# The first feed-forward stage by seven products from its fifth m-tile on, and five modulation sections moved to other stages

## The chip, the cores and the metric

The kernel runs on one core of a Trainium2 chip. Its time is device microseconds of one execution; the kernel before took 2546.53 us (median of three runs, 2545.23 to 2547.19). TensorE multiplies, VectorE and ScalarE do elementwise work, GpSimd is a slower third engine for that, and SyncE (SP in the profile) issues all DMAs.

## The reference, cut to what matters

Two layers run over 640 tokens (128 of a context, 512 latent) of width 1024 in float32. Each layer has a feed-forward stage, a mixer (a recurrent head group and two kinds of attention) and a second feed-forward stage, each with a residual and a layer norm. Shift, scale and gate come from nine "modulation sections" a layer, each 1024 columns of one big matrix, for two condition vectors (one per token group):

```python
mod = (silu(cond) @ w_mod + b_mod)            # 9 sections of 1024 columns
x = layer_norm(ALPHA * x + 0.5*g1 * swiglu(x*(1+sc1)+sh1, lp, 0))
x = layer_norm(ALPHA * x + g2 * mixer(x*(1+sc2)+sh2))
x = layer_norm(ALPHA * x + 0.5*g3 * swiglu(x*(1+sc3)+sh3, lp, 1))
swiglu(u) = (silu(u @ w_gate) * (u @ w_up)) @ w_down     # 1024 -> 2816 -> 1024
```

## The kernel before, in words

**Tiling.** A feed-forward stage works through 22 m-tiles of 128 hidden columns. Every float32 matrix is split into a high and a low part, and a product is three matmuls (high by high, high by low, low by high). In the classic form an m-tile takes, for gate and for up, 8 blocks of the inner dimension by 2 halves of 320 tokens by 3 matmuls: 96 matmuls of 320 columns (`mtile`, the three lines 526 to 528). The down-projection takes groups of m-tiles ("chunks"): for each of 5 token tiles and 2 halves of the output, 3 matmuls of 512 columns per m-tile, 30 per m-tile in all.

**Two forms of the stage.** The first stage of layer 0 is made by `ffn_steps`, all classic, with chunks of 3, 3, 4, 4, 4, 4 (downs at lines 821 to 823). Its down multiplies each result by the gate on VectorE (L828) and adds it to x at once, on GpSimd (L830; VectorE in the last chunk). The three other stages are made by `ffn_fast`: `CLASSIC` = 3 classic m-tiles, and from then on seven products of 4 blocks each instead of eight (a Strassen-like scheme over token halves and inner halves), 7 x 4 x 3 = 84 matmuls per m-tile (L1083). For them VectorE and ScalarE first make sums of the input's quarters (`sums`: two rounds of 11 whole-tile VectorE instructions, high priority), and `third` replaces a quarter in place. Each m-tile's weights are combined and split by `prep` (L1051, L1055, L1059: 4 differences, 7 casts, 7 remainders), and the products' results are put together from six PSUM banks by L1107 to L1137. Downs come after every third m-tile (L1195 to L1197); the sums over m-tiles are gathered without the gate in five tiles `acc` (L1200 copies, then L1208 adds), and `blend`, shortly before the last down, multiplies them by the gate on GpSimd (L1167, ten times) and adds x, which had been written to memory (`x_d`) and is read back (L1165, L1169).

**The opening** is special to layer 0: `start` does m-tiles 0 and 1 while modulation sections 0 and 1 arrive, adding their shift later as a bias (`biased`, with L674 and L687). `start2` does m-tile 2 and between its blocks the eight steps of section 2, on TensorE. VectorE and ScalarE follow the written order until it ends.

**Modulation sections** come in two forms. On TensorE (`body`, L364): 8 steps, each a load of 512 KB and 4 matmuls (which the trace counts as 8 records). On VectorE (`vbody`): 8 steps with a load and 4 instructions each (L329 in the first step, else L331), and at the end matmuls that add over partitions (L340, 16 records). `PLAN` says which sections are made where: in the feed-forward stages by VectorE, in the mixers by TensorE (groups of `MODG` = 4 steps at given units of the attention, `mod_fill`; unit = one head by 128 queries). Eight are in the first stage, two in each mixer, one in each of the others.

**Order.** A stage is a list of `Step`s with loads, splits and a body. `run` traces them in order; at each `yield` of a body (a tick) it makes at most one split of the coming steps, feeds loads while fewer than `NR` = 7 raw buffers are out, and advances the background generators. In `ffn_fast` the sections' VectorE instructions are traced by the generator `trickle`, one per `MGAP` = 12 ticks. A product has 4 ticks, a down 10. A scheduler then orders each engine's instructions by their place in this trace, with `high_priority` moving some ahead; it may start a later instruction when its inputs are there.

Of the kernel before, what the change touches and what calls it, by code (L numbers as in the profile page):

```python
# [18 lines left out]
P = 128  # L19
D = 1024  # L20
KT = 8
# [62 lines left out]
MGAP = 12  # L84
# [3 lines left out]
def f(ap):  # L88
    return ap.bitcast(F32)
# [20 lines left out]
class Kern:  # L110
# [456 lines left out]
    def ffn_steps(self, l, j, mods):  # L567

        nc, I = self.nc, self.I
        env = {}  # L570
        S = []

        def B(dt=F32):
            return env["pool"].tile([P, TOK], dt, tag="B", bufs=11, name=self.nm("b"))

        def DW(shape):
            return env["pool"].tile(shape, F32R, tag="DW", bufs=8, name=self.nm("dw"))

        def T(shape):
            return env["pool"].tile(shape, F32, tag="T", bufs=3, name=self.nm("t"))  # L580

        def G4(shape):
            return env["pool"].tile(shape, F32, tag="G", bufs=4, name=self.nm("g"))

        jj = (0, 2)[j]
        hs = {}
        halves = {}
        dws = []
        for m in range(NM):
            g, u, d = {}, {}, {}  # L590
            fs = slice(m * P, (m + 1) * P)
            halves[m] = (g, u, d)

            def w_in_view(w):
                return w[l, j][:, fs].rearrange("(k p) f -> p k f", p=P)
# [3 lines left out]
            dl, dsp = self.weight(I["ffn_w_down"][l, j][fs, :], [P, D], d, DW)  # L599

            def silu(g, cut=HALF):
                for a, b in self.chunks(g["s"], g["ps"], cut):
                    nc.scalar.activation(a, b, AF.Silu)

            def hout(m, g, u, cut=HALF):
                s = g["s"]
                for a, b in self.chunks(s, u["ps"], cut):
                    nc.vector.tensor_mul(a, a, b)
                hh, hl = B(F32R), B(F32R)
# [4 lines left out]
            dws.append((dl, dsp))  # L614
            late_g, late_d = ((), ()) if m == 0 else LATE[l == 0 and j == 0].get(m, ((), (m,)))

            def gbody(m=m, g=g, late=[fn for i in late_g for fn in dws[i][1]]):
                g["ps"] = self.p2("pg")
                g["s"] = B()
                late = list(late)  # L620
                for c in range(2):
                    for _ in self.mtile(g["ps"], g, c):
                        yield
                        for _ in range(min(2, len(late))):
                            late.pop(0)()
                for fn in late:
                    fn()
                silu(g)


            def ubody(m=m, g=g, u=u, late=[fn for i in late_d for fn in dws[i][1]]):
                u["ps"] = self.p2("pu")
                if l == 0 and j == 0 and m == 4:
                    for i in range(DEPTH):
                        self.setup_vec(i)
                late = list(late)
                for c in range(2):
                    for _ in self.mtile(u["ps"], u, c):
                        yield
                        if late:  # L640
                            late.pop(0)()
                for fn in late:
                    fn()
                hout(m, g, u)

            def first(m=m, g=g, u=u):
                env["cm"] = self.tc.tile_pool(name=f"ffn{l}{j}", bufs=1, reuse_waits="tile")
                env["pool"] = env["cm"].__enter__()
                self.B_DW = DW
                g["ps"], u["ps"] = self.p2("pu"), self.p2()  # L650
                g["s"] = B()
                yield from self.mtile(g["ps"], g, 0, CUT)
                self.after_a()
                yield from self.mtile(u["ps"], u, 0, CUT)
                yield from self.mtile(g["ps"], g, 1, CUT)
                silu(g, CUT)
                yield from self.mtile(u["ps"], u, 1, CUT)
                hout(m, g, u, CUT)

            def biased(m, g, u):  # L660
# [29 lines left out]
                hh, hl = B(F32R), B(F32R)  # L690
                nc.scalar.copy(hh, s)
                nc.vector.tensor_sub(hl, s, f(hh))
                hs[m] = (hh, hl)
# [7 lines left out]
            def start(gsp, usp, g1=g, u1=u):  # L701


                g0, u0, _ = halves[0]
# [24 lines left out]
                env["cm"] = self.tc.tile_pool(name=f"ffn{l}{j}", bufs=1, reuse_waits="tile")  # L729
# [23 lines left out]
            def start2(m=m, g=g, u=u):  # L753
# [4 lines left out]
                for h, k0 in ((g, 0), (u, 0), (g, 4), (u, 4)):  # L758
                    if k0 and self.late_bias:
                        self.bg.append(self.late_bias.pop(0)())  # L760
                    for k in range(k0, k0 + 4):
                        self.block(h, k)
                        yield CAP2 if h is u and k >= 6 else 0
                        if not todo:
                            continue
                        st = todo.popleft()
                        while not st.ready():
                            self.feed()
                        for _ in st.body():
                            yield  # L770
# [1823 lines left out]
```

## Time and profile before

| | us |
|---|---|
| median of three runs | 2546.53 |
| the profiled execution | 2543.89 |
| its span | 2541.8 |
| first feed-forward stage, to the first matmul of the mixer | 537.1 |
| mixer of layer 0, to the first matmul of the next stage | 327.9 |

The page gives, for one profiled execution, the busy time of each engine, the waits and the costliest groups of instructions. PE is TensorE, PEld its weight load, DVE VectorE, ACT ScalarE, POOL GpSimd. A name like L1083 is a line of the kernel. Granted clock is the share of TensorE's full clock.

### The profile page before, as it was taken

What the parts mean: (1) busy time and instruction counts of PE and PEld (TensorE: products, weight loads), DVE (VectorE), ACT (ScalarE), POOL (GpSimd) and SP (SyncE); (2) the same over time, 40 slices, a digit from 0 to 9 for tenths busy, and PEclk for the clock granted to TensorE, in tenths of its full rate; (3) what the DMA queues carried; (4) which work ended last, traced back from release to release, by engine and by line L of the source; (5) the groups of instructions that cost most, each with busy time, mean ns of one, the idle gap of its engine ahead of it and who ended that gap; (6) DMA issues with size and microseconds to landing.
All of it is one profiled execution on the core that took longest, in us unless ns stands there. A gap on an engine that the chain in (4) does not pass through costs nothing. (4 is left out here: it accounts for less than half of the span.)

```text
span 2541.8 us, 39941 instructions
## 1 busy us (share of the span) xinstructions
PE 2443.6 (96%) x15804; PEld 2218.4 (87%) x15804; DVE 1891.1 (74%) x3161; ACT 1068.9 (42%) x1882; POOL 411.2 (16%) x389
## 2 busy tenths in 40 slices
PE   8899999999999999999999999999999999999997
PEld 7789898988867999999889999988987799999986
DVE  5887778687754797777789777778785578777777
ACT  3212111246674444343354434435657534433432
POOL 2320221113632100000200000020373210000022
PEclk9999999999999999999999999999999999999999
DMA  8655445522233233333333333332232323333321
GB/s 286 197 152 155 141 147 185 158 69 80 95 90 113 67 132 111 98 100 100 108 91 124 113 96 100 100 108 82 91 112 90 97 76 100 110 107 104 113 92 50
DMA packets 271394, 288.53 MB, mean 114 GB/s; under 512 B 13436, under 2 KB 223976, under 8 KB 271208
## 3 DMA queue, kind: packets, MB, share of 16 engines
q1 hardware_dynamic: 271208, 285.99, 36.3%
q8 instruction: 124, 2.03, 0.3%
q14 instruction: 62, 0.51, 0.1%
HBM read 268.17 MB, written 16.21 MB: 112 GB/s over the span
## 5 line engine op out<-in xcount | busy, mean ns | idle before, releaser
L1083 PE MATMUL pb<-u,w 128*128 128x320 f32 x2736 | 420.4, 309 | 1.7 <-DVE b L1129 1.7
L1083 PEld LDWEIGHTS pb<-u,w 128*128 128x128 f32 x2736 | 406.7, 188 | 4.0 <-issue 2.4
L526 PE MATMUL p<-u,w 128*128 128x320 f32 (+2 forms) x1104 | 348.3, 316 | 8.6 <-ACT u L517 6.4
L527 PE MATMUL p<-u,w 128*128 128x320 f32 (+2 forms) x1104 | 345.8, 314 | 1.8 <-DVE u L518 1.8
L528 PE MATMUL p<-u,w 128*128 128x320 f32 (+2 forms) x1104 | 344.4, 313 | 0.0
L1083 PE MATMUL pb<-s,w 128*128 128x320 f32 x2052 | 322.0, 309 | 1.3 <-ACT b L1136 1.3
L1083 PEld LDWEIGHTS pb<-s,w 128*128 128x128 f32 x2052 | 306.0, 188 | 3.7 <-ACT b L1136 1.9
L1055 ACT CAST w<-raw 128x512 fp32r<-128x512 f32 x399 | 239.8, 619 | 162.8 <-DVE raw L1051 107.5
L1059 DVE TENSOR_TENSOR w<-raw,w 128x512 fp32r<-128x512 f32 x399 | 272.6, 696 | 34.9 <-ACT w L1055 34.2
L194 ACT CAST dw<-raw 128x1024 fp32r<-128x1024 f32 x87 | 89.1, 1051 | 452.6 <-PE p L1196 263.9
L331 DVE SCALAR_TENSOR_TENSOR x<-raw,cst,x 128x512 f32<-128x512 f32 x308 | 236.9, 815 | 33.3 <-DMA raw<-in_w_mod 33.2
L1195 PE MATMUL p<-dw,b 128*128 128x512 f32 x630 | 249.7, 396 | 11.3 <-DVE x L1208 10.1
L1196 PE MATMUL p<-dw,b 128*128 128x512 f32 x630 | 245.8, 390 | 0.0
L1197 PE MATMUL p<-dw,b 128*128 128x512 f32 x630 | 245.5, 390 | 0.0
L526 PEld LDWEIGHTS p<-u,w 128*128 128x128 f32 x1104 | 211.5, 192 | 13.7 <-ACT u L517 7.4
L527 PEld LDWEIGHTS p<-u,w 128*128 128x128 f32 x1104 | 211.7, 192 | 2.9 <-DVE u L518 2.5
L528 PEld LDWEIGHTS p<-u,w 128*128 128x128 f32 x1104 | 211.1, 192 | 0.3 <-DVE w L199 0.3
L194 ACT CAST w<-raw 128x1024 fp32r<-128x1024 f32 x100 | 104.8, 1050 | 241.3 <-PE p L527 162.3
L1208 DVE TENSOR_TENSOR x<-x,p 128x512 f32<-128x512 f32 x150 | 102.8, 685 | 110.5 <-PE p L1197 110.5
L1195 PEld LDWEIGHTS p<-dw,b 128*128 128x128 f32 x630 | 118.2, 188 | 47.3 <-DVE x L1208 21.6
L199 DVE TENSOR_TENSOR w<-raw,w 128x1024 fp32r<-128x1024 f32 x100 | 124.1, 1242 | 44.6 <-ACT w L194 40.5
L1157 POOL TENSOR_SCALAR x<-x 128x1024 f32<-128x1024 f32 x6 | 6.3, 1056 | 871.1 <-PE p L1197 438.3
(367 smaller groups left out, 4815.7 us busy)
## 6 DMA issues: line engine op xcount, KB each, us to landing
raw<-in_w_mod SPq DMA_DIRECT2D x132, 512.0 KB
raw<-in_ffn_w_gate SPq DMA_DIRECT2D x88, 512.0 KB
raw<-in_ffn_w_up SPq DMA_DIRECT2D x88, 512.0 KB
raw<-in_ffn_w_down SPq DMA_DIRECT2D x88, 512.0 KB
raw<-in_w_in SPq DMA_DIRECT2D x26, 512.0 KB
xd<-x SPq DMA_DIRECT2D x25, 512.0 KB
raw<-in_w_out SPq DMA_DIRECT2D x16, 512.0 KB
t<-xd SPq DMA_DIRECT2D x30, 256.0 KB
```

The source lines that it names most:

```text
L194: nc.scalar.copy(h, hold["raw"])
L199: nc.vector.tensor_sub(l, hold["raw"], f(hold["hi"]))
L331: e.scalar_tensor_tensor(acc[:, cs], hold["raw"][:, cs], c, acc[:, cs], op0=ALU.mult, op1=ALU.add)
L526: nc.tensor.matmul(out, lhsT=wh, rhs=xh, start=start, stop=False)
L527: nc.tensor.matmul(out, lhsT=wh, rhs=xl, start=False, stop=False)
L528: nc.tensor.matmul(out, lhsT=wl, rhs=xh, start=False, stop=stop)
L1055: nc.scalar.copy(w[:, 0], at(src))
L1059: nc.vector.tensor_sub(w[:, 1], at(src), f(w[:, 0]))
L1083: nc.tensor.matmul(out, lhsT=a1, rhs=b1, start=(start and k == 0 and i == 0), stop=(k == 3 and i == 2), skip_group_check=not start,)
L1195: nc.tensor.matmul(pt, lhsT=hh[:, ts], rhs=d["hi"][:, cs], start=(i == 0), stop=False)
L1196: nc.tensor.matmul(pt, lhsT=hh[:, ts], rhs=d["lo"][:, cs], start=False, stop=False)
L1197: nc.tensor.matmul(pt, lhsT=hl[:, ts], rhs=d["hi"][:, cs], start=False, stop=(i == len(ms) - 1))
```

## The change

`ffn_steps` goes. Its special parts for m-tiles 0 to 2 become `opening`, and the first stage is now made by `ffn_fast` too, with four classic m-tiles (`classic = CLASSIC + opens`), so from m-tile 4 on by seven products. The order at the start is: `start`; `third` (m-tile 2, no section between its blocks); the gate half of m-tile 3, at whose beginning the sums are started; the splits of the first three down weights; the down of m-tiles 0 to 2, copied into `acc` without the gate; the up half of m-tile 3; then the products. At the end of `third` the five x tiles are written to memory, for the blend before the last down. The pool of the stage has 10 tiles `B` and 6 `DW` (11 and 8 before); m-tile 2's weights still use four of the `DW`.

Section 2 of layer 0 moves from m-tile 2 (TensorE) into the first stage's list (VectorE). From that list, sections 5, 6 and 7 of layer 0 and section 0 of layer 1 go to mixer 0, and sections 1 and 2 of layer 1 to the second feed-forward stage. Of layer 1, section 3 moves from mixer 0, and section 4 from the second stage, to the third feed-forward stage, and section 5 from there to mixer 1. So the first stage has three sections in its list instead of eight, mixer 0 five instead of two, mixer 1 three instead of two, and the second and third feed-forward stages two each instead of one. The gap of `trickle` now depends on the number of sections in the stage. Its core:

```diff
 PLAN = {
-    "f00": [[], [], [(0, 3), (0, 4), (0, 5), (0, 6), (0, 7), (1, 0), (1, 1), (1, 2)]],
-    "m0": [[], [(0, 8), (1, 3)]],
-    "f01": [[], [], [(1, 4)]],
-    "f10": [[], [], [(1, 5)]],
-    "m1": [[], [(1, 6), (1, 7)]],
+    "f00": [[], [], [(0, 2), (0, 3), (0, 4)]],
+    "m0": [[], [(0, 5), (0, 6), (0, 7), (0, 8), (1, 0)]],
+    "f01": [[], [], [(1, 1), (1, 2)]],
+    "f10": [[], [], [(1, 3), (1, 4)]],
+    "m1": [[], [(1, 5), (1, 6), (1, 7)]],
     "f11": [[], [], [(1, 8)]],
 }
-MGAP = 12
+MGAP = 12, 11, 5, 3
...
-    def ffn_steps(self, l, j, mods):
+    def opening(self, env, hs, B, DW):
...
-            def start2(m=m, g=g, u=u):
+            def third(m=m, g=g, u=u):
                 g["ps"], u["ps"] = self.p2(), self.p2()
                 g["s"] = B()
-                todo = deque(self.next_steps)
                 for h, k0 in ((g, 0), (u, 0), (g, 4), (u, 4)):
                     if k0 and self.late_bias:
                         self.bg.append(self.late_bias.pop(0)())
                     for k in range(k0, k0 + 4):
                         self.block(h, k)
                         yield CAP2 if h is u and k >= 6 else 0
-                        if not todo:
-                            continue
-                        st = todo.popleft()
-                        while not st.ready():
-                            self.feed()
-                        for _ in st.body():
-                            yield
...
+                self.order.__exit__(None, None, None)
+                self.x_d = [self.dp.tile([P, D], F32, name=self.nm("xd")) for _ in range(NT)]
+                for t in range(NT):
+                    nc.sync.dma_start(out=self.x_d[t], in_=self.x[t])
...
+        opens = l == 0 and j == 0
+        classic = CLASSIC + opens
...
             def gate():
+                if opens:
+                    env["sums"] = sums()
+                    self.bg.append(env["sums"])
...
         S = []
-        for m in range(CLASSIC):
+        if opens:
+            S += self.opening(env, hs, B, DW)
+            gate, up = plain(3)
+            for m in range(3):
+                dl, dsp = down_w(m)
+                gate.loads.append(dl)
+                S.append(Step([], dsp))
+            S[-3:] = [gate] + S[-3:] + [down([0, 1, 2], begin=True), up]
+        for m in range(0 if opens else CLASSIC):
...
+        gap = MGAP[sum(len(v) for v in mods.values()) // KT]
...
-                        for _ in range(MGAP):
+                        for _ in range(gap):
                             yield
...
-        seq = [("A", CLASSIC), ("A", CLASSIC + 1), ("D", 2)]
-        for m in range(CLASSIC, NM):
+        seq = [("A", classic), ("A", classic + 1)] + ([] if opens else [("D", 2)])
+        for m in range(classic, NM):
...
-            plan = spread(PLAN[f"f{l}0"], *((4,) if l == 0 else (4, 16)))
-            new = self.ffn_steps(l, 0, plan) if l == 0 else self.ffn_fast(l, 0, plan)
+            plan = spread(PLAN[f"f{l}0"], *((5, 17) if l == 0 else (4, 16)))
+            new = self.ffn_fast(l, 0, plan)
```

## Rows read from the trace of the kernel before

**Rows 1.** The page, busy us, share of the span and instructions.
```profile
PE 2443.6 (96%) x15804; PEld 2218.4 (87%) x15804; DVE 1891.1 (74%) x3161; ACT 1068.9 (42%) x1882; POOL 411.2 (16%) x389
```
**Rows 2.** Windows: start:end, length; busy (instructions) PE PEld DVE ACT POOL; clock; DMA.
```profile
86.83:95.99 9.16, 9.16 (x50) 8.83 (x49) 9.16 (x15) 3.08 (x5) 0.00 (x0) 0.77 0.78 244
95.99:122.67 26.68, 22.35 (x92) 16.35 (x91) 26.18 (x27) 3.08 (x4) 13.79 (x8) 1.00 0.38 114
122.67:505.45 382.78, 376.75 (x2370) 348.69 (x2368) 287.70 (x396) 79.13 (x90) 63.80 (x43) 1.00 0.51 157
505.45:537.10 31.65, 31.08 (x156) 25.78 (x153) 27.67 (x56) 13.69 (x29) 3.42 (x8) 1.00 0.11 29
537.10:865.00 327.90, 309.79 (x2329) 272.06 (x2328) 217.83 (x443) 191.53 (x353) 115.91 (x118) 0.97 0.27 87
```
**Rows 3.** TensorE's waits, 55 to 540: us in total, times, longest.
```profile
PE p L821 <- DVE t L828: 10.3, 15, 1.3
PE p L679 <- DVE b L674: 4.5, 1, 4.5
```
**Rows 4.** TensorE's timeline: start us, us, instruction.
```profile
499.95 0.31 PE L526 MATMUL p<-u,w 128*128 128x320 f32 x1
...
504.21 0.31 PE L528 MATMUL p<-u,w 128*128 128x320 f32 x1
504.45 1.07 PE L340 MATMUL p<-x,sel 128*32 128x256 f32 x16
505.45 0.50 PE L821 MATMUL p<-dw,b 128*128 128x512 f32 x1
```
**Rows 5.** Windows of the second feed-forward stage, products and downs.
```profile
1002.67:1039.63 36.96, 36.96 (x254) 36.95 (x252) 33.41 (x55) 19.82 (x39) 0.00 (x0) 1.00 0.41 116
1039.63:1060.70 21.07, 20.76 (x93) 16.83 (x92) 11.22 (x19) 2.59 (x5) 0.00 (x0) 1.00 0.25 72
1157.00:1177.60 20.60, 20.60 (x94) 17.06 (x93) 9.49 (x21) 2.46 (x4) 1.06 (x1) 1.00 0.18 64
1177.60:1214.60 37.00, 37.00 (x254) 36.94 (x253) 30.41 (x49) 19.81 (x39) 0.00 (x0) 1.00 0.38 112
1214.60:1239.70 25.10, 22.52 (x93) 16.35 (x92) 13.95 (x24) 2.36 (x4) 10.66 (x8) 1.00 0.30 97
1279.20:1311.80 32.60, 31.55 (x155) 25.57 (x153) 28.68 (x58) 15.62 (x31) 2.93 (x4) 1.00 0.09 27
```
**Rows 6.** VectorE's timeline in the second stage.
```profile
1033.29 1.41 DVE L331 SCALAR_TENSOR_TENSOR x<-raw,cst,x 128x512 f32<-128x512 f32 x2
1034.61 0.48 DVE L1132 TENSOR_TENSOR b<-b,pb 128x320 f32<-128x320 f32 x1
1035.01 1.89 DVE L1059 TENSOR_TENSOR w<-raw,w 128x512 fp32r<-128x512 f32 x3
1036.82 0.49 DVE L1137 TENSOR_TENSOR b<-b,b 128x320 f32<-128x320 f32 x1
```
**Rows 7.** VectorE's timeline around the first down of the first stage.
```profile
84.88 1.28 DVE L329 TENSOR_SCALAR x<-raw,cst 128x512 f32<-128x512 f32 x3 [4.90 <-DMA raw<-in_w_mod]
86.07 0.41 DVE L674 COPY b<-p 4x256 f32<-4x256 f32 x1
...
98.93 2.44 DVE L331 SCALAR_TENSOR_TENSOR x<-raw,cst,x 128x512 f32<-128x512 f32 x2
```
**Rows 8.** Groups by line: busy us, mean ns, idle before.
```profile
L830 POOL TENSOR_TENSOR x<-x,t 128x512 f32<-128x512 f32 x50 | 77.3, 1548 | 297.4 <-DVE t L828 297.2
L1167 POOL TENSOR_TENSOR x<-x,x 128x512 f32<-128x512 f32 x30 | 42.4, 1414 | 205.6 <-DVE x L1208 205.6
L982 DVE TENSOR_TENSOR b<-u,u 128x640 f32<-128x640 f32 x24 | 18.7, 819 | 0.0
```
**Rows 9.** Windows of L364 alone, mixer 0's attention, four units each.
```profile
706.66:715.37 8.71, 0.00 (x0) 0.00 (x0) 1.00 0.09 21
...
727.11:739.15 12.04, 3.82 (x46) 1.34 (x46) 1.00 0.68 218
```

More of the change, by code (lines that the diff above doesn't have):

```diff
@@ L612, in hout @@
                 hs[m] = (hh, hl)
[L614 to L622, printed above, removed]
-                        yield
[L624 to L658, printed above, removed]
             def biased(m, g, u):
@@ L689, in biased @@
                     )
[L690 to L693, printed above, removed]
+                parts(m, s, lambda: B(F32R))
             def kept(g, u):
@@ L701, in start @@
             def start(gsp, usp, g1=g, u1=u):
-                g0, u0, _ = halves[0]
+                g0, u0 = halves[0]
                 lo, hi = range(4), range(4, 8)
@@ L728, in start @@
                 blocks(u0, hi)
-                env["cm"] = self.tc.tile_pool(name=f"ffn{l}{j}", bufs=1, reuse_waits="tile")
+                env["cm"] = self.tc.tile_pool(name="ffn00", bufs=1, reuse_waits="tile")
                 env["pool"] = env["cm"].__enter__()
@@ L841, in ffn_steps @@
-        out = []
-        m0 = 0
-        chunk_end = {}
-        for ci, n in enumerate(CHUNKS):
-            ms = list(range(m0, m0 + n))
-            chunk_end[m0 + n - 1] = (ci, ms)
-            m0 += n
-        pos = 0
-        m = 0
-        pend = None
-        while pos < len(S):
-            if m == 0:
-                out.append(S[pos])
-                pos += 1
-            else:
-                out.append(S[pos])
-                if pend is not None:
-                    out.append(down(*pend))
-                    pend = None
-                out.append(S[pos + 1])
-                pos += 2
-            nmod = len(mods.get(m, []))
-            out.extend(S[pos : pos + nmod])
-            pos += nmod
-            if m in chunk_end:
-                pend = chunk_end[m]
-            m += 1
@@ L869, in ffn_steps @@
-        out.append(down(*pend))
-        return out
+                S.append(Step([gl, ul], gsp + usp, third, 0))
+        return S
     def ffn_fast(self, l, j, mods):
@@ L1174, in body @@
                 if begin:
-                    for _ in self.res:
+                    for _ in () if opens else self.res:
                         pass
@@ L1222, in ffn_fast @@
         S = []
-        for m in range(CLASSIC):
+        if opens:
+            S += self.opening(env, hs, B, DW)
+            gate, up = plain(3)
+            for m in range(3):
+                dl, dsp = down_w(m)
[3 more added lines that the diff above has]
+        for m in range(0 if opens else CLASSIC):
             st = plain(m)
@@ L1229, in ffn_fast @@
             S += st + mods.get(m, [])
-        dl, dsp = down_w(CLASSIC - 1)
+        dl, dsp = down_w(classic - 1)
         S[-1].loads.append(dl)
@@ L1262, in rest, with vecs @@
             yield
-        seq = [("A", CLASSIC), ("A", CLASSIC + 1), ("D", 2)]
-        for m in range(CLASSIC, NM):
+        def vecs():
+            for i in range(DEPTH):
+                self.setup_vec(i)
+            yield
+        seq = [("A", classic), ("A", classic + 1)] + ([] if opens else [("D", 2)])
+        for m in range(classic, NM):
             seq.append(("B", m))
@@ L1275, in ffn_fast @@
                 S += part_a(m)
+                if opens and m == classic:
+                    S.append(Step([], [], vecs))
             elif what == "B":
```

101 lines of the change are left out of this document (15 added, 86 removed).

## The prediction, made before the changed kernel was run

> **What bounds the kernel now.** I read the page first. TensorE is busy for 96% of the span, VectorE for 74%, and no other engine for half of it [rows 1]. Then came busy time by stage, with borders from TensorE's timeline [rows 2]. The first feed-forward stage ends at 537.10. In its long stretch from 122.67 to 505.45 TensorE is busy for 376.75 of 382.78 us, and the reader should see that nothing but work on that engine is worth time there. Before it lie a slow piece of 9.16 us at a mean granted clock of 0.77 (between the levels 1.2 and 2.4 GHz) and the first down-projection, 26.68 us with 4.33 us idle. TensorE's waits say why [rows 3]: 15 times, 10.3 us in all, it waited for VectorE's gate product L828 to empty a bank; once, for 4.45 us, for the copy L674, just before the slow piece.
>
> The price of TensorE's work is the distance between starts, since busy times of pipelined matmuls overlap. From 499.95 to 504.21 lie 29 distances: 0.1469 us per matmul of 320 columns; the 16 records that end a VectorE-made section take 1.00 us until the next start [rows 4]. In the stage that has seven products already, 90 down matmuls take 20.60 us less some 0.15 for two transposes, 0.2272 each, and the product stretch 1177.60 to 1214.60 holds 252 matmuls, 0.1468 each [rows 5].
>
> **The main stretch.** Before, 122.67 to 505.45 holds the up half of m-tile 3 (48 matmuls), 18 m-tiles of 96, 15 m-tiles' downs (450) and eight section ends: 260.9 + 102.2 + 8.0 = 371.1; the other 11.7 us are waits and changes of kind. After it holds 48 + 18 x 84 matmuls, the same 450, and three ends: 229.2 + 102.2 + 3.0 = 334.4. The stage at 916 to 1279 spends almost nothing between kinds except where its blend runs: its down there takes 25.10 us where another takes 20.60, so +4.5 [rows 5]. The last classic up half now stands directly before the first product, with no down between to hide VectorE emptying its bank: one 128x640 product and a bank handover, +1.5 (0 to 3.5). On SP the stage issues 48 section loads fewer and five writes of x, ten reads of it and two gate rows more; the second stage hides the same reads and rows but for the 4.5, so they cost nothing beside it. That makes 340.4, and 42.4 us gone, if VectorE follows.
>
> **Does VectorE follow?** A period of three m-tiles and a down takes it 30.41 + 9.49 = 39.9 us without a section and 33.41 + 11.22 = 44.6 with one section trickling, of 57.5 [rows 5]. Three sections over twelve m-tiles are 24 instructions a period. Two L331 in a row take 1.32 us from start to start, 0.66 each [rows 6]: 15.8 us, so 55.7 of 57.5. Back to back the rest shrinks a little, since three L1059 take 1.81 instead of 3 x 0.69 [rows 6], to some 53. So it fits, barely, but only if the sections slip into the downs: a product stretch of 37.0 us already holds 30.41, and 21 of the 24 instructions are issued there (84 of its 94 ticks are the products'). If none slips, a product stretch needs 30.41 + 13.9 = 44.3 and the four periods lose 29 us; if all slip, nothing is lost. The weights are prepared three products, 5.3 us, ahead, and the one-section rows show TensorE full at 36.96 of 36.96 with VectorE at 33.41, nearer to the cheap end. I take 8. The same raw ring of seven now also holds two section loads per m-tile, which brings the up weights later; that is in the 8. Main stretch: -34.
>
> **GpSimd.** The 50 adds L830, 1548 ns each, go [rows 8]; beside one, two L331 took 2.44 us instead of 1.41 [rows 6, 7]. That is why I price L331 by the second stage. Ten products L1167 of 1414 ns come with the blend [rows 8]; their cost is inside the 4.5.
> The Trainium skill (page "SBUF — State Buffer", section "Who interferes with whom") says that a VectorE instruction with two inputs in SBUF is shut out while a GpSimd instruction that reads SBUF holds the shared ports, for that whole instruction. By that rule the ten L1167 could shut VectorE out for 14.1 us; if TensorE waited through all of it, the sum would end 9.6 us later. The down beside the blend shows 4.5, so I keep the row.
>
> **The opening.** Section 2 leaves m-tile 2. Its TensorE form costs 64 records; in the attention 46 of them stretched four units from 8.71 to 12.04 us [rows 9], 0.0724 each, so 4.6. Its eight loads of 512 KB leave the queue ahead of m-tile 3's gate weights. The 4.45 us wait was L674, queued on VectorE behind L329, which sat 4.90 us for a section's load [rows 7]; no section is near now. The slow piece is 48 matmuls that should take 7.05: 2.1 lost. The first down should take 20.5: 6.2 lost, mostly L828 slowed beside GpSimd; ScalarE copies L1200 replace it there. All together 17.4. Against it stand the sums (24 instructions like L982, 819 ns [rows 8], some 18 us packed, at high priority) that must be done within m-tile 3 and the first down, 34.6 us, together with some 12 us of splits, biases and products, and two of the three down weights can be split only when m-tile 2's weights free their buffers (6 instead of 8). Also five x tiles must be written to memory before the down may take their buffers. I take 5.4 of the 17.4 as lost to these: -12, bounds -17.4 and +5.
>
> **The tail and the mixers.** The last down of a seven-product stage takes 32.60 against 31.65 [rows 2, 5]: +1. Mixer 0 gets three more sections and mixer 1 one, all on TensorE in the attention, where TensorE is the bound: the 46 records lengthened the units by 3.33 us, all of it seen [rows 9]. 4 x 64 x 0.0724 = 18.5. Filling gaps (309.79 busy of 327.90 in mixer 0 [rows 2]) could give back up to 4; a section also holds one of the two banks that the attention's values need, up to +8. I take +1.5: 20. The ten groups bring 20 MB of loads; some 2 MB per 9.5 us is below what the opening moved (244 GB/s in the slow piece), so I cost them at nothing.
>
> **The two stages with a second section.** Each gets one more section end, 1.0, and VectorE goes from 44.6 to about 50 of 57.5. By the same two bounds, 0 and 10 each, 2: together +6. The last stage's gap of 11 instead of 12: nothing.
>
> **The sum.** -34 - 12 + 1 + 20 + 6 = -19. The profiled execution took 2543.89 (span 2541.8 and 2.1 around it), 2.6 below the median of the runs; 2543.9 - 19 = 2525, set against the median 2546.5: **2527**.
>
> **Rivals.**
> A, cover holds everywhere: the sections slip into the downs (nothing lost in three stages), the opening gives its full amount. -42 - 16 + 1 + 18.5 + 2 = -36: 2510. For it: full TensorE with one section; against it: VectorE at 96%.
> B, no gain is left: VectorE spends the opening on the sums first, so the first down starts no earlier (0 instead of -12), and the attention loses 6 more to the held bank: -1, 2545. For it: VectorE busy for 26.18 of 26.68 in the first down already [rows 2]; against it: those were L331 beside GpSimd.
> C, slower: VectorE becomes the bound in the product stretches. The sections' instructions are issued evenly in the products' ticks and, once queued, stand ahead of later preparations; if they don't slip into the downs, a stretch of 37.0 becomes 44.3 four times in the first stage (29), and with two sections 30.41 + 9.2 = 39.6, four times in each of two stages (21). That is 50 where the sum has 12: 2565. It decides from 27 us more than the sum, some 2.3 us per m-tile with sections. Against it: with one section only 3.0 of the 4.7 us fell into the products [rows 5].
> That the products would not be fewer I exclude: the loop from m-tile 4 on issues 84 for 96.
>
> **How the numbers follow.** Forecast 0.58, A 0.18, B 0.12, C 0.12. The forecast's own range is 2515 to 2540. Down to 2508 takes in the greater part of A, up to 2550 all of B; C and the rest of A stay out, so 2508 to 2550. A measurement of this kernel tells some 0.2%, 5 us, from no change: faster is below 2541.4. That holds nearly all of the forecast (0.56), A and a little of B (0.03): 0.77. B's middle gives 0.10 for no change, and C with the upper edge 0.13 for slower.
>
> **What would show it.** The stretch from the first product to the last down lasts some 340 us (332 without loss); VectorE is above 92% busy in its middle; waits of L1083 for L1059 or for up weights stay under 10 us. M-tile 3's gate starts near 77 us and at full clock. Mixer 0 grows by 14 to 16 us, mixer 1 by 5. The prediction is wrong if product stretches last over 39 us (C), if the first down still starts at 96 (B), or if the mixers grow by much less than 18, since then the gaps of the attention hide sections.

## The result and the profile after

The changed kernel takes 2516.6 us in the median (2514.74 to 2519.84, four runs), the kernel before 2545.88 in the same comparison: ratio 0.9886, 95% interval 0.9869 to 0.9903. Forecast were 2527 and 2508 to 2550. A second comparison gave 0.9898 (0.9884 to 0.9913). The profiled execution took 2519.84 us (span 2518.0), 24.05 less than that of before; the medians differ by 29.3, because before's profiled execution is its fastest and this one the slowest of its four.

The page, busy us, share and instructions, as in [rows 1]: 72 matmul records fewer, VectorE busier.

```profile
PE 2418.0 (96%) x15732; PEld 2186.4 (87%) x15732; DVE 1934.2 (77%) x3333; ACT 1135.9 (45%) x2062; POOL 347.0 (14%) x347
```

Windows of the changed kernel, columns as in [rows 2]: from the gate half of m-tile 3 to the first product, from there to the last down, the last down, mixer 0, mixer 1.

```profile
83.80:121.20 37.40, 35.48 (x188) 30.92 (x187) 35.00 (x54) 19.81 (x31) 0.00 (x0) 1.00 0.15 43
121.20:460.33 339.13, 333.69 (x2018) 307.12 (x2016) 287.97 (x474) 134.62 (x247) 16.64 (x12) 1.00 0.45 134
460.33:492.87 32.54, 31.50 (x154) 25.52 (x153) 28.62 (x58) 15.58 (x31) 4.01 (x8) 1.00 0.14 38
492.87:829.39 336.52, 321.13 (x2525) 275.42 (x2524) 221.48 (x452) 190.82 (x352) 115.45 (x118) 0.98 0.38 124
...
1733.52:2061.56 328.04, 310.65 (x2396) 270.34 (x2394) 220.69 (x450) 190.74 (x352) 115.25 (x118) 0.99 0.32 102
```

The first stage ends at 492.87 instead of 537.10, mixer 0 is 336.52 long instead of 327.90 [rows 2]. TensorE's waits in 55 to 540, as in [rows 3] (L595, L1042, L930, L906 are L666, L1195, L1083, L1059 of before): the waits for the gate product and for L674 are gone, the first row is new, and the products wait 2.3 us in all.

```profile
PE p L595 <- DVE shr L2316: 4.8, 1, 4.8
PE p L506 <- ACT x L496: 3.2, 2, 2.3
PE p L1042 <- DVE x L1055: 2.5, 7, 0.4
...
PE pb L930 <- DVE w L906: 0.9, 2, 0.5
PE pb L930 <- ACT w L902: 0.9, 2, 0.7
PE pb L930 <- DVE b L976: 0.5, 1, 0.5
```

Stage by stage, from TensorE's timelines, in us. The stages are the first feed-forward stage (F1), mixer 0 (M0), the second and third (F2, F3), mixer 1 (M1), and the fourth to the end of the span (F4).

| kernel | F1 | M0 | F2 | F3 | M1 | F4 |
|---|---|---|---|---|---|---|
| before | 537.1 | 327.9 | 446.8 | 444.7 | 325.6 | 459.7 |
| after | 492.9 | 336.5 | 452.4 | 451.7 | 328.0 | 456.4 |
| after, again (e5) | 492.1 | 335.6 | 447.4 | 446.5 | 328.7 | 456.5 |
| sections alone (e1) | 517.4 | 338.7 | 450.7 | 445.6 | 328.2 | 456.9 |
| five sections (e2) | 536.8 | 328.2 | 447.6 | 446.3 | 336.1 | 455.9 |
| section 2 back (e3) | 488.0 | 337.4 | 449.5 | 446.2 | 332.4 | 458.0 |
| mixers' two blocks (e4) | 492.3 | 327.2 | 449.3 | 448.0 | 333.2 | 457.8 |
| sums in order (e6) | 488.8 | 335.9 | 448.2 | 448.1 | 331.1 | 456.4 |
| light sections (e7) | 490.1 | 337.0 | 449.3 | 447.1 | 330.2 | 454.8 |
| mixers twice (e8) | 493.8 | 353.7 | 449.5 | 447.5 | 347.6 | 458.1 |
| back and in order (e9) | 487.8 | 337.1 | 450.1 | 447.6 | 329.5 | 457.2 |
| blend on VectorE (e10) | 485.1 | 338.1 | 443.2 | 441.8 | 331.2 | 451.6 |
| blend on GpSimd (e11) | 491.8 | 336.2 | 448.3 | 447.7 | 332.1 | 456.7 |
| all (e12) | 486.2 | 332.1 | 443.4 | 441.6 | 333.4 | 452.6 |

How far a stage repeats is read from kernels that do the same there. M0 with its five sections is 335.6 to 338.7, and F2 and F3 differ by some 5 between the two traces of the changed kernel. M1 with its three sections runs from 328.0 to 336.1, and F1 inherits up to 2 us from the start of m-tile 3's gate (82.45 to 84.36 in the twelve traces that open with `third`, with or without section 2 in it). And the levels differ: beside e1 to e12 the kernel before took 2537.8 to 2539.5 us in the median, 6 to 8 less than beside the first result, and it has no trace from there. Ratios are safe from that, differences from before's row are not.

### The profile page after: what moved, and what is told of

The parts are those of the page before. It is cut to its first block, busy times and chain, and to the rows that moved or that the text cites. A ratio compares the mean times of both kernels' runs of the same rounds, so it can differ in the third digit from the quotient of the medians.

```text
span 2518.0 us, 40146 instructions
## 1 busy us (share of the span) xinstructions
PE 2418.0 (96%) x15732; PEld 2186.4 (87%) x15732; DVE 1934.2 (77%) x3333; ACT 1135.9 (45%) x2062; POOL 347.0 (14%) x347
## 5 line engine op out<-in xcount | busy, mean ns | idle before, releaser
L930 PE MATMUL pb<-u,w 128*128 128x320 f32 x3600 | 554.6, 309 | 2.2 <-DVE b L976 2.2
L930 PEld LDWEIGHTS pb<-u,w 128*128 128x128 f32 x3600 | 534.8, 188 | 7.0 <-issue 4.6
L930 PE MATMUL pb<-s,w 128*128 128x320 f32 x2700 | 424.4, 310 | 2.0 <-DVE w L906 0.9
L902 ACT CAST w<-raw 128x512 fp32r<-128x512 f32 x525 | 315.9, 619 | 230.6 <-DVE raw L898 151.6
L930 PEld LDWEIGHTS pb<-s,w 128*128 128x128 f32 x2700 | 402.4, 188 | 7.1 <-DVE w L906 1.8
L906 DVE TENSOR_TENSOR w<-raw,w 128x512 fp32r<-128x512 f32 x525 | 357.0, 692 | 45.8 <-ACT w L902 44.4
L1042 PE MATMUL p<-dw,b 128*128 128x512 f32 x830 | 330.3, 398 | 18.8 <-DVE x L1055 16.7
L1043 PE MATMUL p<-dw,b 128*128 128x512 f32 x830 | 324.5, 391 | 0.0
L1044 PE MATMUL p<-dw,b 128*128 128x512 f32 x830 | 324.2, 391 | 0.0
L1042 PEld LDWEIGHTS p<-dw,b 128*128 128x128 f32 x830 | 156.1, 188 | 68.4 <-DVE x L1055 34.5
L1055 DVE TENSOR_TENSOR x<-x,p 128x512 f32<-128x512 f32 x200 | 136.5, 682 | 86.2 <-PE p L1044 85.6
L1044 PEld LDWEIGHTS p<-dw,b 128*128 128x128 f32 x830 | 156.2, 188 | 33.3
L1043 PEld LDWEIGHTS p<-dw,b 128*128 128x128 f32 x830 | 156.3, 188 | 29.2
L331 DVE SCALAR_TENSOR_TENSOR x<-raw,cst,x 128x512 f32<-128x512 f32 x224 | 163.6, 751 | 19.5 <-DMA raw<-in_w_mod 19.5
L526 PE MATMUL p<-u,w 128*128 128x320 f32 (+2 forms) x528 | 167.1, 318 | 7.4 <-ACT u L517 7.4
L527 PE MATMUL p<-u,w 128*128 128x320 f32 (+2 forms) x528 | 166.4, 317 | 1.5 <-DVE u L518 1.4
L528 PE MATMUL p<-u,w 128*128 128x320 f32 (+2 forms) x528 | 164.8, 314 | 0.0
L199 DVE TENSOR_TENSOR dw<-raw,dw 128x1024 fp32r<-128x1024 f32 x86 | 105.3, 1228 | 41.9 <-ACT dw L194 41.7
L898 DVE TENSOR_TENSOR raw<-raw,raw 128x512 f32<-128x512 f32 x150 | 103.0, 687 | 10.6 <-DMA raw<-in_ffn_w_up 8.7
```

Of the source, the lines that this page charges most:

```text
L199: nc.vector.tensor_sub(l, hold["raw"], f(hold["hi"]))
L331: e.scalar_tensor_tensor(acc[:, cs], hold["raw"][:, cs], c, acc[:, cs], op0=ALU.mult, op1=ALU.add)
L526: nc.tensor.matmul(out, lhsT=wh, rhs=xh, start=start, stop=False)
L527: nc.tensor.matmul(out, lhsT=wh, rhs=xl, start=False, stop=False)
L528: nc.tensor.matmul(out, lhsT=wl, rhs=xh, start=False, stop=stop)
L902: nc.scalar.copy(w[:, 0], at(src))
```

## The experiments

**e1 and e2: is it the products or the moved sections?** e1 leaves the first stage classic and moves only the sections (section 2 stays on TensorE).

```diff
-    "f00": [[], [], [(0, 3), (0, 4), (0, 5), (0, 6), (0, 7), (1, 0), (1, 1), (1, 2)]],
+    "f00": [[], [], [(0, 3), (0, 4)]],
+    # other stages and the gaps as in the changed kernel
```

> The kernel before with the new places of the sections (section 2 stays on TensorE in m-tile 2) and the new gaps, but the first stage still classic. If the price of the move is what the two profiles show (mixer 0 +8.6, mixer 1 +2.4, second and third feed-forward stage +5.7 and +7.0: 23.7 in all) and the classic first stage gets back its six section ends (6.0) and half or all of its 11.7 us of waits, the median is 2546 + 24 - 12 to - 18 = 2552 to 2558, with mixer 0 at 336 to 337 us. Rival, that the classic stage was held up by VectorE and the move alone is what pays: 2535 or less. Second rival, that these prices belong to the new first stage (what it leaves behind) and not to the sections: mixers and stages as before, 2530 to 2540.

Measured: ratio 0.9997 (0.9988 to 1.0006). F1 20 us shorter, M0 and M1 13 longer, F2 and F3 5. The moves alone give nothing. (Six sections leave the first stage's list in the change; the title's five is the net of section 2's arrival.) None of the three expectations came: F1 gave a little more than its ends and all its waits (17.7), and the other stages cost 18 instead of 23.7.

e2 is the changed kernel with two of the moved sections back in the first stage's list.

```diff
-    "f00": [[], [], [(0, 2), (0, 3), (0, 4)]],
-    "m0": [[], [(0, 5), (0, 6), (0, 7), (0, 8), (1, 0)]],
+    "f00": [[], [], [(0, 2), (0, 3), (0, 4), (0, 6), (0, 7)]],
+    "m0": [[], [(0, 5), (0, 8), (1, 0)]],
-MGAP = 12, 11, 5, 3
+MGAP = 12, 11, 5, 3, 1, 1
```

> The changed kernel with five sections instead of three in the first stage (6 and 7 of layer 0 come back from mixer 0; one of their instructions at every tick). If VectorE is close to full there (about 53 to 56 us of 57.5 in a period with three sections), 16 more instructions a period of 0.66 us need 10.6 us a period that it has not got: four periods, 30 to 40 us longer in the first stage, less 6 in mixer 0: 2540 to 2552, with VectorE near 100% busy and TensorE waiting for weights. Rival, that VectorE has room because sections slip into the downs and the last m-tiles: first stage less than 8 us longer, 2512 to 2520.

Measured: ratio 1.0048 (1.0035 to 1.0062). F1 is 536.8, as long as with the classic form: the products' whole gain is gone (30 to 40 us were expected, 44 came). TensorE's waits in e2's first stage, and two windows of it (columns as in [rows 2]):

```profile
PE pb L930 <- ACT w L902: 13.6, 14, 2.0
PE pb L930 <- DVE w L906: 8.4, 13, 1.0
```
```profile
335.36:345.40 10.04, 8.19 (x55) 7.66 (x54) 10.04 (x19) 1.49 (x3) 1.21 (x1) 1.00 0.78 237
345.40:355.40 10.00, 5.33 (x21) 4.14 (x20) 8.28 (x13) 3.57 (x6) 0.00 (x0) 0.82 0.54 163
```

The waits add up to 22 us, half of the 44. VectorE is busy for 10.04 of 10.04 us in the first window and 8.28 of 10.00 in the second, TensorE is idle for 18% and then 47%, and its granted clock goes from 1.00 to a mean of 0.82, between 2.4 and 1.2 GHz: part of the rest is slower matmuls. So the loss that rival C feared is real, two sections away. That VectorE alone makes it isn't shown: in the products ScalarE's casts L902 waited 60.2 us for VectorE's differences L898, but also 33.6 for loads of gate weights, and the gap of 1 instead of 3 came with the two sections and wasn't tried alone.

**e3: section 2 back on TensorE**, between m-tile 2's blocks, with two sections left in the list.

```diff
-    "f00": [[], [], [(0, 2), (0, 3), (0, 4)]],
+    "f00": [[], [], [(0, 3), (0, 4)]],
                     for k in range(k0, k0 + 4):
                         self.block(h, k)
                         yield CAP2 if h is u and k >= 6 else 0
+                        # one step of section 2, as in start2 before
```

> The changed kernel with section 2 again on TensorE between the blocks of m-tile 2 (its eight loads ahead of m-tile 3's weights), and two sections in the first stage's list. If the section's 4.6 us on TensorE lay beside VectorE's chain of shifts, which TensorE now waits 4.85 us for, they cost nothing here: gate of m-tile 3 within 2 us of the changed kernel's 83.8 unless its weights come late, and the stretch of products 2 to 5 us shorter with less on VectorE: 2510 to 2516. Rival, that the opening pays for the section as the prediction had it (4.6 on TensorE and the wait for late loads, up to 10): gate at 88 to 94, 2519 to 2526.

Measured: ratio 0.9896 (0.9882 to 0.9909), the same as after. M-tile 3's gate starts at 83.26, no later than the 83.80 without the section, the first product at 120.67. So section 2's 4.6 us of TensorE cost nothing there; of F1's 4 to 5 us less, 3.1 to 4.3 come from the products, where the third section's VectorE work and its end are gone.

**e4: what the mixers' sections cost.** Only the first and the last of a section's eight blocks are multiplied; six are left out of the sum, loads and evictions stay.

```diff
-                for c in range(4):
+                for c in range(4 if k in (0, KT - 1) else 0):
```

> The changed kernel, with the mixers' sections multiplying only their first and last of eight blocks (six are loaded and left out of the sum). 48 of 64 TensorE records go from each of five sections in mixer 0 and three in mixer 1: 17.4 and 10.4 us at 0.0724 each. If the attention pays for them in full, mixer 0 becomes 17 us shorter (319), mixer 1 10 (318), median 2489. If it hides part of them, as mixer 0's 8.6 us for three sections say (2.9 each instead of 4.6), 11 and 6.5 us, median 2499. If what it pays is mainly the held bank or the loads, under 5 us in all: 2512 or more.

Measured: ratio 0.9876 (0.9861 to 0.9891). M0 is 8.4 to 9.3 shorter for 240 records fewer, 0.037 each, half of the price in [rows 9]; M1 is not shorter (333.2) for 144 fewer, but 144 at that price are 5 us, less than M1's spread.

**e5 to e8, on one chip.** e5 is the changed kernel itself.

> The changed kernel once more, beside the experiments of this call. Expected of every theory: the same ratio as the first time, 0.987 to 0.990. It shows how far the lengths of the stages differ between two profiled executions of one kernel: I expect under 2 us for the first stage and mixer 0, up to 6 us for the other four stages. If the second and third feed-forward stages come out 4 us shorter than the first time, their growth of 12.6 us was partly scatter; if they are within 1 us of it, it belongs to the kernel.

Measured: 2513.48, ratio 0.9898. F2 and F3 are 5.0 and 5.2 shorter than in the first trace of the same program, so most of their growth of 12.6 there was not the kernel's.

e6 takes the sums' high priority away in the first stage.

```diff
-                with self.tc.high_priority(offset=SUMS):
+                with self.tc.high_priority(offset=0 if opens else SUMS):
```

> The sums of the first stage lose their high priority and stand on VectorE in the order in which they are traced. Theory (the sums take VectorE just when the first down needs the product of m-tile 2 and its weights' splits, so the opening gave 8.5 us instead of 12): the first product starts 1 to 3.5 us earlier than 121.2, the first stage is 1 to 3.5 us shorter, all else is equal. Rival (the sums have to be done before the products anyway, and 18 us of them fit nowhere else): the first product waits for the last sum instead, the stage is 0 to 5 us longer. Third possibility: nothing moves, because the down is held by m-tile 2's weights freeing their buffers and not by VectorE's order.

VectorE's timeline after (start, us, instruction) has the sums L829 to L848 in front and m-tile 2's remainder L586, which the first down needs, behind them:

```profile
89.46 2.29 DVE L829 TENSOR_TENSOR b<-u,u 128x640 f32<-128x640 f32 x3
...
101.96 0.82 DVE L841 TENSOR_TENSOR b<-b,b 128x640 f32<-128x640 f32 x1
102.70 0.82 DVE L586 TENSOR_TENSOR x<-b,x 128x640 fp32r<-128x640 f32 x1
```

In e6 it comes 12 us earlier, and from the start of the gate half (82.71) to the first product TensorE is busy for all of 34.70 us, where after's 37.40 hold 1.92 of idle time; the products then take as long as after's:

```profile
90.57 0.82 DVE L586 TENSOR_TENSOR x<-b,x 128x640 fp32r<-128x640 f32 x1
```
```profile
82.71:117.41 34.70, 34.70 (x191) 31.15 (x189) 34.03 (x52) 19.22 (x31) 0.00 (x0) 1.00 0.28 86
117.41:456.26 338.85, 333.06 (x2017) 307.01 (x2016) 288.62 (x476) 134.63 (x248) 16.59 (x12) 1.00 0.42 131
```

So the sums' priority costs 2.7 us, as expected. F1 is 3.3 shorter than e5's. The ratio, 0.9889 (0.9875 to 0.9902), can't tell 3 us.

e7 leaves out VectorE's instructions for six of eight blocks of the three sections.

```diff
-                        else:
+                        elif not (l == 0 and s <= 4 and 0 < k < KT - 1):
```

> Left out are the VectorE instructions of six of the eight blocks of the three sections of the first stage (72 instructions, some 47 us of VectorE); loads and section ends stay. Theory (VectorE's shortage in the product stretches costs what the prediction took, 8 us of the 339 from the first product to the last down): the stretch falls to 331 to 333, the first stage to 485 to 487, the time by 6 to 8 us. Rival 1 (the 11.8 us above the counted work are the blend, the handover and kinds that change, and VectorE costs nothing with three sections): the stretch stays within 2 us of 339. Rival 2 (rows of before and of the changed kernel have VectorE's share twice, once as waits on the last remainder and once as late downs): it falls by more than 10.

```profile
121.09:457.57 336.48, 331.36 (x2018) 307.30 (x2016) 247.03 (x404) 133.71 (x247) 16.25 (x12) 1.00 0.43 134
```

VectorE does 41 us less, and the stretch is 2.65 us shorter (ratio 0.9891, 0.9878 to 0.9905). With three sections VectorE's shortage is some 3 us (1.5 against e5's stretch of 337.93), nearer to rival 1 than to the 8 taken.

e8 issues each of the mixers' section matmuls twice.

```diff
-                for c in range(4):
+                for c in range(4 if not late else 8):
+                    c, _ = c % 4, c // 4
```

> Every matmul of the sections in the two mixers is issued twice (320 records more in mixer 0, 192 in mixer 1); loads, evictions and order stay. Theory of the prediction (each record is seen in full, 0.0724 us): mixer 0 grows by 23 us, mixer 1 by 14, the time by 37. Rival, from the two-block run (0.039 us a record in mixer 0, nothing in mixer 1, because TensorE's idle pieces in the attention take part of them): mixer 0 grows by 12.5, mixer 1 by 0 to 7, the time by 13 to 20. Third: the gaps near the sections are used up by the first set, then the growth is the full 37 although the first set cost half.

Measured: ratio 1.0028 (1.0016 to 1.0041), 33.9 us over e5 for 512 records, 0.066 each. M0 in e8 and in e5 (two kernels, same columns):

```profile
493.78:847.52 353.74, 339.17 (x2846) 285.11 (x2844) 222.63 (x452) 190.95 (x352) 115.33 (x118) 0.99 0.36 118
```
```profile
492.11:827.73 335.62, 320.92 (x2525) 275.61 (x2524) 222.15 (x452) 190.62 (x352) 115.32 (x118) 0.98 0.38 125
```

M0 grows by 18.1 (0.057 a record) with the same 14.6 us of idle TensorE as e5's 14.7; before it was 18.1 [rows 2]. M1 grows by 18.9, more than its 192 records at full price (13.9); its spread is in that. The third possibility is the nearest: the first records find room, later ones cost almost the price in [rows 9].

**e9: e3 and e6 together** (both diffs above).

> Both cheap findings on the opening in one kernel: section 2 back on TensorE between m-tile 2's blocks (two sections left in the first stage's list), and the sums in their traced order. Theory (the two are independent: the first took 4.8 us off the first stage, the second 3.3 to 4.0): the first stage ends at 484 to 485 instead of 492 to 493, the time is 8 us below the changed kernel, ratio some 0.9865 against 0.9898. Rival (both only give VectorE the same 4 us of the opening, and the second one finds them taken): the stage ends at 487 to 488, the ratio stays at 0.988 to 0.989.

Measured: ratio 0.9893 (0.9879 to 0.9908), F1 487.8. The number is the rival's: beside e6, moving section 2 back gives 1 us more, not 4. Its reason isn't: from the gate half to the first product e9 takes e6's 34.70, so the opening's gain is not taken twice. The products take 336.84, 2.0 less than in e6 (e3: 3.1 to 4.3 less), and the gate starts 1.05 later than in e6, within its spread.

**e10 and e11: the blend.** What of the 339.13 us is no counted work? Windows after: two product stretches and the down between them and the blend, then the down and the stretch with the blend.

```profile
178.75:218.63 39.88, 39.22 (x269) 37.37 (x268) 35.25 (x60) 18.77 (x37) 0.00 (x0) 1.00 0.50 149
...
299.61:336.56 36.95, 36.95 (x253) 36.95 (x252) 36.09 (x60) 20.75 (x39) 0.00 (x0) 1.00 0.50 155
336.56:356.99 20.43, 20.43 (x93) 16.90 (x91) 10.65 (x18) 2.44 (x4) 0.00 (x0) 1.00 0.15 50
...
395.36:420.44 25.08, 22.54 (x92) 16.35 (x91) 13.94 (x24) 2.35 (x4) 10.65 (x8) 1.00 0.30 92
420.44:460.33 39.89, 39.22 (x266) 38.72 (x264) 31.14 (x48) 20.68 (x37) 3.49 (x2) 1.00 0.50 142
```

The down beside the blend takes 4.65 us more than the other. The timeline of all engines inside it shows a round that repeats every 2.69 us, where nine matmuls of 512 columns take 2.04:

```profile
402.11 0.50 PE L1042 MATMUL p<-dw,b 128*128 128x512 f32 x1 [0.44 <-DVE x L1055]
402.13 1.29 POOL L1014 TENSOR_TENSOR x<-x,x 128x512 f32<-128x512 f32 x1 [1.40 <-DVE x L1055]
403.45 0.69 DVE L1016 TENSOR_TENSOR x<-x,t 128x512 f32<-128x512 f32 x1 [1.40 <-POOL x L1014]
404.06 0.68 DVE L1055 TENSOR_TENSOR x<-x,p 128x512 f32<-128x512 f32 x1
404.80 0.50 PE L1042 MATMUL p<-dw,b 128*128 128x512 f32 x1 [0.34 <-DVE x L1055]
```

The brackets are idle time and who ended it. VectorE waits in its order for GpSimd's product; the add that empties TensorE's bank stands behind that wait. e10 moves the multiplication to VectorE, e11 instead the add to GpSimd, each in all four stages.

```diff
# e10
-                    nc.gpsimd.tensor_mul(acc[t][:, cs], acc[t][:, cs], g[:, cs])
+                    nc.vector.tensor_mul(acc[t][:, cs], acc[t][:, cs], g[:, cs])
# e11
-                    nc.vector.tensor_add(acc[t][:, cs], acc[t][:, cs], xin)
+                    nc.gpsimd.tensor_add(acc[t][:, cs], acc[t][:, cs], xin)
```

> The blend's ten multiplications go from GpSimd to VectorE, in all four feed-forward stages. Theory (the last but one down and the product stretch after it last 25.1 and 39.9 us instead of 20.4 and 37.0 because per half tile an add into acc, the multiplication on GpSimd and the add of x stand one behind the other in VectorE's order, 2.69 us where the down needs 2.04): with 0.68 us for the multiplication on VectorE the down lasts 20.5 to 22, the stretch 37 to 38, each stage is 4 to 7 us shorter, the four together 16 to 28. Rival (VectorE is short there anyway, and three instructions of 0.68 per half tile are again 2.04): down at 22 to 24, the late preparations lengthen the next stretch to 39 to 42, the time is the same. Second rival (x read back from memory or the gate rows come late): both stretches stay as they are.

> The opposite: the blend's ten adds of x go from VectorE to GpSimd too, in all four stages, so VectorE waits for nothing of the blend. Theory (the cost is VectorE's wait in order for GpSimd, 12.4 us in each stage): the down falls to 20.5 to 22 us and the stretch after it to 37 to 39, the time by 12 to 25. Rival (the cost is that GpSimd's instructions slow VectorE's down while they run, and there are now twice as many of them, some 26 us a stage): the down stays at 24 or more, the stretch grows beyond 40, the time is 0 to 20 us longer.

The same two windows in e10, then in e11:

```profile
393.40:413.83 20.43, 20.43 (x92) 16.90 (x91) 19.87 (x33) 2.33 (x4) 0.00 (x0) 1.00 0.36 116
413.83:452.55 38.72, 38.72 (x266) 38.71 (x264) 30.76 (x49) 20.80 (x37) 0.00 (x0) 1.00 0.51 146
```
```profile
394.45:414.88 20.43, 20.43 (x93) 16.89 (x91) 9.89 (x17) 2.34 (x4) 16.21 (x13) 1.00 0.27 88
414.88:459.29 44.41, 40.78 (x266) 40.26 (x264) 33.65 (x45) 20.90 (x37) 12.94 (x8) 0.96 0.48 140
```

e10: ratio 0.9824 (0.9809 to 0.9838). Both windows have TensorE full. F1 is 7.0 to 7.8 shorter, of which 1.4 to 1.8 are the gate's earlier start, long before the blend; F2, F3 and F4 are 4 to 5 shorter each (against e5). The theory holds. e11: ratio 0.9908 (0.9892 to 0.9925), no gain: theory for the down, rival for the stretch. The down is at its 20.43 with GpSimd busy for 16.21 us of it, so there the cost was VectorE's wait and not GpSimd's running beside it. But the stretch takes 5.7 us more than e10's. Its long wait, 3.04 us, goes back to a load:

```profile
422.59 8.13 SPq L189 DMA_DIRECT2D raw<-in_ffn_w_down  x2
428.06 1.04 ACT L194 CAST dw<-raw 128x1024 fp32r<-128x1024 f32 x1 [7.09 <-DMA raw<-in_ffn_w_down]
429.01 0.43 ACT L983 ACTIVATE b<-pb 128x320 f32<-128x320 f32 x1
429.49 3.34 PE L930 MATMUL pb<-s,w 128*128 128x320 f32 x12 [3.04 <-ACT b L983]
```

On SP the last reads of x (L1012) wait for GpSimd's adds to free their buffers (25.6 us in eight waits), and the down weight's load stands behind them: it is issued 7.7 us after the stretch's start, in e10 3.0 (416.84). ScalarE sits for it, and L983, which empties TensorE's bank, stands behind that. In the 10 us from 430 on the granted clock is a mean of 0.84.

**e12: e10, e9 and section 5 of layer 0 back from mixer 0** in the first stage's list.

> The parts that helped, together: the blend's multiplications on VectorE, section 2 on TensorE between m-tile 2's blocks, the sums in their traced order, and section 5 of layer 0 back from mixer 0 into the first stage's list, which again holds three sections for VectorE. Theory (VectorE has room for three sections in the first stage, where they cost 2 to 3 us, each section in mixer 0 costs 2.9, the blend's gain lies elsewhere): first stage 481 to 483 us, mixer 0 333 to 335, the time 3 to 6 us below the kernel with the blend alone, ratio 0.980 to 0.981. Rival (the opening's 4 us come back in the products, where VectorE now also does the blend's multiplications): first stage 485 or more, ratio 0.982 or above.

Measured: 2486.24, ratio 0.9792 (0.9778 to 0.9806), the fastest of all; 0.3% below e10. M0 is 332.1, a little below the theory's figure. F1 is 486.2, the rival's: one down of it (274.41 to 298.94), with the third section running, takes 24.53 instead of 20.43. The opening kept its gain (34.70 again); against e10 the gate starts 0.85 later and the stretch to the last down is 2.9 longer (335.61 against 332.72), most of it in that down. VectorE is busy for 18.93 us of the 24.53, and what TensorE waits for there goes back to a late load of gate weights:

```profile
280.26 0.62 ACT L910 CAST w<-raw 128x512 fp32r<-128x512 f32 x1 [3.21 <-DMA raw<-in_ffn_w_gate]
280.91 0.69 DVE L914 TENSOR_TENSOR w<-raw,w 128x512 fp32r<-128x512 f32 x1 [2.68 <-ACT w L910]
282.92 0.71 PE L1050 MATMUL p<-dw,b 128*128 128x512 f32 x1 [2.20 <-DVE x L1063]
```

In the 6 us from 284 on the granted clock is a mean of 0.80. Whether the sections' loads make that load late wasn't tried, and the profiled execution is 4.8 us above e12's median, so the others may not have it. The time fell by 8 us against e10, more than the theory's 3 to 6; the two intervals are wide enough for that difference.

## Why the prediction was right, step by step

The range and the direction held and the main term was right; its two corrections and the terms of the opening, the mixers and the middle stages were off in size. They were off in both directions, so that the number came within 11 us of the forecast is in part luck. In us, against before's trace, for the two traces of the changed kernel:

| step | forecast | after | e5 |
|---|---|---|---|
| main stretch (first product to last down) | -34 | -36.6 | -37.8 |
| opening | -12 | -8.5 | -8.0 |
| last down | +1 | +0.9 | +0.9 |
| mixers | +20 | +11.1 | +10.8 |
| second and third stage | +6 | +12.6 | +2.4 |
| last stage | 0 | -3.3 | -3.2 |

**Main stretch.** From m-tile 4 to the last down before took 375.75 us (129.70 to 505.45), after 339.13; the forecast was 340, against 332 without loss. The window ahead of it, from the gate half of m-tile 3, is in before:

```profile
86.83:129.70 42.87, 38.54 (x187) 32.20 (x187) 42.37 (x48) 6.73 (x9) 17.74 (x10) 0.95 0.50 149
```

The 84 for 96 matmuls came as counted. But its two corrections were mis-sized against each other: 8 for VectorE's shortage was 1.5 to 2.7 (e7), and 4.5 for the blend was 5.8 in the two windows (4.65 in the down, 1.17 in the next stretch, 39.89 against 38.72 in e10), 5.2 to 6.4 over the whole stretch. The smaller part could be read from the borders of [rows 5], 1239.70 to 1279.20, 39.5 long: the prediction read the down beside the blend and not the stretch behind it.

**Does VectorE follow?** Yes, as forecast "barely": from 158.54 to 336.56 it is busy for 166.05 of 178.02 us, 93%, up to 36.09 of 36.95 in one stretch. Most of the sections' instructions did fit, the cheap one of the two bounds. Rival C's 44 us a stretch didn't come. Two stretches crossed the 39 us that the prediction set for C: 39.89 beside the blend, and 39.88 with a section's end in it, where e7, light on VectorE, takes 38.15. So of C's 7 us a stretch under 2 came, once. With five sections, in e2, one stretch takes 54.66 (322.89 to 377.55).

**Opening.** The step "Section 2 leaves m-tile 2", worth 4.6 us, failed. The section and the 4.45 us wait for L674 did go, some 9 us together, yet m-tile 3's gate starts at 83.80 instead of 86.83 and not near 77: 3 us came. What was late next is the first row of the waits above, 4.85 us before the shift's matmuls L595: their operand `shr` comes from a chain of VectorE and ScalarE (L2307, L2308, L2315, L2316), which was there before and which the section's work had covered (e3: with the section, no such wait and no later start). From the gate half to the first product it was the other way round: 5.5 us came (37.40 instead of 42.87), and "I take 5.4 as lost" to the sums and the rest was twice too much. With high priority the sums put L586 at 102.70, so TensorE began the down, left it for the up half and came back; e6, e9 and e12, without the priority, take 34.70, so that costs 2.7. (L828, put down as slowed beside GpSimd, took 0.68 us there, at 98.32 and 101.30; slowed were the two L331 between them, [rows 7].) Rival B (no gain, 0) named the sums' mechanism; it gave 8.5 and not 0, since the up half filled most of the hole.

**Mixers.** "In full, all of it seen" is the step that was wrong by most: 8.6 and 2.4 us for four sections where 18.5 were taken, and the 1.5 for the held bank, which no row priced, not seen. "The mixers grow by much less than 18" was one of the prediction's own signs of being wrong. M1's part can't be sized: its spread is 8 us. M0's can, since six amounts of section work were run in it:

| TensorE records of sections in M0 | 80 (e4) | 128 (before) | 192 (e2) | 256 (e12) | 320 (nine traces) | 640 (e8) |
|---|---|---|---|---|---|---|
| M0, us | 327.2 | 327.9 | 328.2 | 332.1 | 335.6 to 338.7 | 353.7 |

Up to 192 records they cost nothing that these traces can tell; from there on they cost 0.05 to 0.07 each, near the 0.0724 of [rows 9]. So the third section was free and the fourth and fifth cost about 4 and 5 us, close to the 4.6 taken. [rows 9] is a stretch of the attention with TensorE full; the mixer as a whole had 18.1 us without it. Where the first records found room is not shown: only 2.7 of these 18.1 were filled. The other amounts have one trace each, and F1 or the blocks left out differ between these kernels.

**The two middle stages.** +12.6 in one trace, +2.4 in another of the same program. Eight more kernels do the same in these stages (e1 to e4, e6 to e9): +2.4 to +6.2. Against before's one trace, taken while it ran 7 us slower, that fits the 6 and doesn't prove it.

**Last stage.** It is 3 us shorter in both traces, and 2.8 in e1, which shares only its gap of 11. That fits the gap, but it wasn't tried alone, and the stage's spread over e1 to e9 and e11 is as large (454.7 to 458.1).

**The two parts need each other.** The moves alone give 0.9997, the products with five sections 1.0048, both together 0.9886: the classic form leaves VectorE room that the products use up. The products with all eight sections were not run. The forecast had this in its check on VectorE, not as a price.

## What to carry over

A removed TensorE step pays only if no other engine's chain ends at the same place: list what is late next before the gain is booked. When one engine's order holds an instruction that waits for a slower engine, look at what stands behind it: here one moved multiplication (ratio 0.9824 against 0.9886 and 0.9898) gave 16 to 19 us, over half of what the whole change had given. And the price of an addition need not be constant: here the third section of a mixer was free and the later ones cost almost what a stretch without idle time had shown. Neither that stretch nor an average over several sections prices each.

## What was not expected of the hardware

GpSimd beside VectorE slows only some of its instructions. In e11, VectorE's L1055, which reads one operand from PSUM, takes 0.69 us beside GpSimd's adds, as it does alone; L906 and L898, with operands in SBUF only, take up to 1.78 and 1.67 instead of 0.69, and GpSimd's own take up to 2.28 instead of 1.29:

```profile
402.51 1.29 POOL L1016 TENSOR_TENSOR x<-x,t 128x512 f32<-128x512 f32 x1
402.84 0.69 DVE L1055 TENSOR_TENSOR x<-x,p 128x512 f32<-128x512 f32 x1 [1.35 <-PE p L1044]
...
417.72 2.28 POOL L1014 TENSOR_TENSOR x<-x,x 128x512 f32<-128x512 f32 x1
...
420.59 1.67 DVE L898 TENSOR_TENSOR raw<-raw 128x512 f32<-128x512 f32 x1
422.19 1.78 DVE L906 TENSOR_TENSOR w<-raw,w 128x512 fp32r<-128x512 f32 x1
```

The Trainium skill (page "SBUF — State Buffer", section "Who interferes with whom") has the two engines share one pair of SBUF ports, held by one of them at a time; these rows agree. That e11's down is free fits it too: what VectorE does there for the down is L1055.
